# A decoder trunk on one core: the split of a state-space quarter moved behind the scan's loops, and its 20 small transfers begun by POOL

## The chip, the cores and the metric

One core of one Trainium2 chip runs the whole program. The metric is the device time of one execution in microseconds (us), as the median of several runs. The engines are named as in the profile: PE (TensorE, matrix products; PEld its weight loads), DVE (VectorE), ACT (ScalarE), POOL (GpSimd) and SP (SyncE, which in this kernel begins nearly all transfers; SPq is its queue).

## The reference

One layer of a decoder trunk over 1024 tokens and 1024 channels in float32. One projection of the normed input feeds three mixers, whose results are gated, summed and projected; a gated feed-forward block follows. The change touches only the state-space mixer:

```python
def s5_mixer(u, lam_re, lam_im, b_re, b_im, c_re, c_im, d_skip, log_dt, w_glu):
    ...
    lam_bar = jnp.exp(lam * dt)
    b_bar = ((lam_bar - 1.0) / lam)[..., None] * b
    bu = jnp.einsum('bsgh,gph->bsgp', uf.astype(jnp.complex64), b_bar)
    ...
    _, states = lax.associative_scan(combine, (a, bu), axis=1)
    y = jnp.einsum('bsgp,ghp->bsgh', states, c).real + d_skip * uf
    y = jax.nn.gelu(y.reshape(bsz, seq, SSM_WIDTH)).astype(u.dtype)
    y_lin, y_gate = jnp.split(y @ w_glu, 2, axis=-1)
    return y_lin * jax.nn.sigmoid(y_gate)
```

There are 32 groups of 16 channels with 64 complex states each: 512 channels in all.

## The kernel before, in words

All large products run in float32r as three matrix products: each operand is split into a high part (made by ACT, L61) and a low part (made by DVE as the difference, L62), and high x high, low x high and high x low are summed (L120, L122, L124). Weights arrive as `raw`, begun by SP at L83, and are split into `whi` and `wlo`; up to three weight blocks are split ahead of use. Nearly all tiles of 128 x 1024 floats share one pool of 44 pages.

The state-space mixer works in four quarters (q = 0 to 3) of 8 groups. For each, `s5` (L1102 and on) calls these steps:

- `s5_kernel`: PE makes the 8-step kernel (L979), ACT and DVE write it into `kz` (L983, L987), and 8 transfers (L991, 64 KB each) spread it into the page M.
- `s5_carry`: 4 transfers (L968, 128 KB each) move the coefficients into the page cp.
- `s5_back` (from q = 1 on): 8 transfers (L1084, 64 KB each) bring the result of the quarter before from DRAM into the page yT, with the time steps regrouped.
- `s5_inputs`: PE transposes (L1002), ACT writes the page Bm (L1005).
- `s5_parts` (from q = 1 on): ACT and DVE split yT into `mhi` and `mlo`, for the product with `w_glu` at the very end of the stage.
- `s5_scan`: PE makes the inputs of the states (L1015); DVE and ACT copy them to the page V (L1024, L1022); DVE makes products and sums (L1031 to L1035) and eight scans (L1039), then the state page X (L1048 to L1054), which POOL has cleared in its first column (L1044).
- `s5_tables` of the next quarter on DVE, then `s5_out`: PE sums M x U (L1066) and cp x X (L1070), ACT applies GELU (L1073), and SP begins the store `sy` (L1076).

Beside the quarters runs a filler, a generator that yields after each large matrix product: first the short convolution (`conv_rows`), whose blocks give `cb` (L719), `z` (L722), a POOL product of both (L726), `cy` on ACT and DVE (L727 to L729), and a second POOL product (L734); then the last input block (`u_block(3)`, `ut` at L683), then the mixing products of convolution and attention (`mix_plain`), whose sums DVE evacuates at L1166 and adds at L1170. `fill(n)` takes n steps of it; within the scan's loops `beat` takes 3.5 steps at a time, 5 in the last quarter. After the drain of the filler comes `mix_ssm`, which reads the four pairs `mhi`, `mlo` of the quarters.

In this stage PE runs in the written order (`manual_schedule`). The order on the other engines is chosen by a planner when the program is made; each engine then runs its instructions in that order, each waiting for its data. A tile's page comes free when its last reader is done. POOL begins no transfer in the kernel before.

```python
    def beat(self):
        self.due += self.F5B
        self.fill(int(self.due))
        self.due -= int(self.due)
...
    with tc.manual_schedule(engines={mybir.EngineType.PE}):
        k.fill(24)
        k.s5()
        k.drain()
```

Of the kernel before, what the change touches and what calls it, by code (L numbers as in the profile page):

```python
# [15 lines left out]
P = 128  # L16
# [17 lines left out]
class Trunk:  # L34
# [203 lines left out]
    def kv_rows(self):  # L238
# [7 lines left out]
        W = [self.weights() for _ in range(5)]  # L246
        A, B = (W[0], W[2]), (W[1], W[3], W[4])
        for t in range(NT):
            ps = self.wide()
            tok = slice(t * P, (t + 1) * P)  # L250
            for k in range(KD):
                a, b = A[k // 4], B[k // 3]
                ca, cb = slice((k % 4) * 256, (k % 4) * 256 + 256), slice((k % 3) * 280, (k % 3) * 280 + 280)
# [16 lines left out]
            nc.vector.tensor_tensor(sq[:, :256], kr, kr, op=OP.mult)  # L270
            nc.vector.tensor_reduce(self.ssk[:, t], sq[:, :256].rearrange("p (n d) -> p n d", d=64), axis=AX.X, op=OP.add)
            if t > 4:
# [34 lines left out]
    def q_rows(self):  # L307
# [3 lines left out]
        for t in range(NT):  # L311
# [8 lines left out]
            nc.vector.tensor_tensor(sq, q, q, op=OP.mult)  # L320
            nc.vector.tensor_reduce(self.ssq[:, t], sq.rearrange("p (n d) -> p n d", d=64), axis=AX.X, op=OP.add)
            self.q.append(q)
# [41 lines left out]
    def compress(self):  # L364
# [27 lines left out]
        for which in range(2):  # L392
# [25 lines left out]
            nc.vector.tensor_tensor(sv, kv, kv, op=OP.mult)  # L418
            nc.vector.tensor_reduce(ss, sv, axis=AX.X, op=OP.add)
            self.rstd(ss)  # L420
# [39 lines left out]
    def cmp_scores(self, t):  # L460
# [11 lines left out]
        m, sm = st[:, 0:8], st[:, 8:16]  # L472
        nc.vector.tensor_reduce(m, v, axis=AX.X, op=OP.max)
        nc.vector.tensor_tensor(v, v, m[:, :, None].to_broadcast([P, 8, 32]), op=OP.subtract)
        nc.scalar.activation(v, v, AF.Exp)
        nc.vector.tensor_tensor(v, v, self.seen[:, t, None, :].to_broadcast([P, 8, 32]), op=OP.mult)
        nc.vector.tensor_reduce(sm, v, axis=AX.X, op=OP.add)
        nc.vector.tensor_scalar(sm, sm, 1e-30, None, op0=OP.max)
# [110 lines left out]
    credit, t = 0.0, 0  # L589
# [88 lines left out]
    def u_block(self, q, beside=None):  # L678
# [9 lines left out]
        nc.sync.dma_start(spill, ut)  # L688
        self.U[q] = U = self.page("UT").rearrange("p (g n) -> p g n", g=8)
        nc.sync.dma_start(U, spill.rearrange("(g h) j n -> (h j) g n", g=8))  # L690

    def u_blocks(self):

        self.tab, self.U = {}, {}

# [267 lines left out]
    def s5_carry(self, cr):  # L963

        cp = self.page("cp").rearrange("p (a g c) -> p a g c", a=4, g=2)
        for c in range(2):
            for g in range(2):
                self.nc.sync.dma_start(cp[c * 64:(c + 1) * 64, :, g].rearrange("p a (d h) -> p a d h", h=16),  # L968
                                       cr[c][g * 64:g * 64 + 64, :, 0:8])
        return cp  # L970

    def s5_kernel(self, q, cr, bb):

        nc = self.nc
        M = self.page("M").rearrange("p (a g c) -> p a g c", a=4, g=2)
        ps = self.acc()
        for a in range(4):
            for c in range(2):
                nc.tensor.matmul(ps[:32, a * P:(a + 1) * P], bb[:, c, a].rearrange("p g h -> p (g h)"),  # L979
                                 cr[c][:, a, 1:9].rearrange("p d h -> p (d h)"), start=c == 0, stop=c == 1)  # L980
        kz = self.page("kz")[:32, :960].rearrange("p (a c) -> p a c", a=4)
        nc.gpsimd.memset(kz[:, :, 128:240], 0.0)
        nc.scalar.activation(kz[:, :, 0:128], ps[:32].rearrange("p (a c) -> p a c", a=4), AF.Copy)  # L983
        dd = self.half("dd")[:32, :64].rearrange("p (a h) -> p a h", a=4)
        nc.vector.tensor_tensor(dd, self.eye2[:, None, :].to_broadcast([32, 4, 16]),
                                self.dT[:, 4 * q:4 * q + 4, None].to_broadcast([32, 4, 16]), op=OP.mult)
        nc.vector.tensor_tensor(kz[:, :, 112:128], kz[:, :, 112:128], dd, op=OP.add)  # L987
        for g in range(2):
            for a in range(4):
                x = kz[g * 16:(g + 1) * 16, a]  # L990
                nc.sync.dma_start(M[:, a, g], bass.AP(x.tensor, x.offset, [list(x.ap[0]), [16, 8], [1, P]]))  # L991
        self.fill(self.F5)
        return M

    def s5_inputs(self, q, bp):

        nc = self.nc
        B = self.page("Bm").rearrange("p (a g c s) -> p a g c s", a=4, g=2, c=2)
        ps = self.wide()
# [4 lines left out]
        for c in range(2):  # L1004
            nc.scalar.activation(B[:, :, :, c], ps.rearrange("p (j c g s) -> p c j g s", j=4, c=2, g=2)[:, c], AF.Copy)  # L1005
        self.fill(2 * self.F5)
        return B

    def s5_scan(self, q, U, B, ep):
        nc = self.nc  # L1010
        v = nc.vector
        V = self.page("V5").rearrange("p (c a n) -> p c a n", c=2, a=4)
        ps = self.wide()
        for j in range(8):
            nc.tensor.matmul(ps[:, j * P:(j + 1) * P], B[:, j // 2, j % 2].rearrange("p c s -> p (c s)"), U[:, j],  # L1015
                             start=True, stop=True)
        pv = ps.rearrange("p (a g n) -> p g a n", a=4, g=2)
        for g in range(2):
            for c in range(2):
                o = V[g * 64:(g + 1) * 64, c]  # L1020
                if c:
                    nc.scalar.activation(o, pv[c * 64:(c + 1) * 64, g], AF.Copy)  # L1022
                else:
                    nc.vector.tensor_copy(o, pv[c * 64:(c + 1) * 64, g])  # L1024
        self.fill(2 * self.F5)
        f = lambda x: x.rearrange("p a n -> p (a n)")
        vr, vi, ec, es = f(V[:, 0]), f(V[:, 1]), f(ep[:, 0]), f(ep[:, 1])
        t = [self.half("m5") for _ in range(3)]
        a, b = self.half("a5"), self.half("b5")
        for o, z, x0, x1, op in ((b, t[2], vi, vr, OP.subtract), (a, t[0], vr, vi, OP.add)):  # L1030
            v.tensor_tensor(z, x0, ec, op=OP.mult)  # L1031
            self.beat()
            v.tensor_tensor(t[1], x1, es, op=OP.mult)
            self.beat()
            v.tensor_tensor(z, z, t[1], op=op)  # L1035
            self.beat()
            for j in range(4):
                s = slice(j * P, (j + 1) * P)
                v.tensor_tensor_scan(o[:, s], self.mag8[:, 4 * q + j:4 * q + j + 1].to_broadcast([P, P]), z[:, s], 0.0,  # L1039
                                     op0=OP.mult, op1=OP.add)  # L1040
                if j % 2:
                    self.beat()
        X = self.page("X5").rearrange("p (a g n) -> p a g n", a=4, g=2)
        nc.gpsimd.memset(X[:, :, :, 0:1], 0.0)  # L1044
        w = lambda x: x.rearrange("p (a n) -> p a n", a=4)[:, :, 0:127]
        ec, es = ep[:, 0, :, 0:127], ep[:, 1, :, 0:127]
        for c, x0, x1, op in ((0, a, b, OP.subtract), (1, b, a, OP.add)):
            v.tensor_tensor(w(t[0]), w(x0), ec, op=OP.mult)  # L1048
            self.beat()
            v.tensor_tensor(w(t[1]), w(x1), es, op=OP.mult)  # L1050
            self.beat()
            for g in range(2):
                pr = slice(g * 64, g * 64 + 64)
                v.tensor_tensor(X[c * 64:(c + 1) * 64, :, g, 1:], w(t[0])[pr], w(t[1])[pr], op=op)  # L1054
                self.beat()
        return X

    def s5_out(self, q, U, M, X, cp):

# [18 lines left out]
    def s5_back(self):  # L1078

        nc, spill = self.nc, self.spill_y  # L1080
        yT = self.page("yT").rearrange("p (t n) -> p t n", t=8)
        back = spill.rearrange("(t h) g n -> t g h n", t=8)
        for t in range(8):
            nc.sync.dma_start(yT[:, t], back[7 - t])  # L1084
        self.last = yT

    def s5_parts(self):
# [14 lines left out]
    def s5(self):  # L1102
        self.yT = []
        tab = self.tab
        for q in range(4):
            bp, cr, bb, ep = tab.pop(q)
            M = self.s5_kernel(q, cr, bb)
            cp = self.s5_carry(cr)
            U = self.U[q]
            if q:  # L1110
                self.s5_back()
            B = self.s5_inputs(q, bp)
            if q:
                self.s5_parts()
            self.F5B = 3.5 if q < 3 else 5
            X = self.s5_scan(q, U, B, ep)
            if q < 3:
                for _ in self.s5_tables(q + 1, tab):
                    self.beat()
            self.fill(self.F5S)  # L1120
            self.s5_out(q, U, M, X, cp)
        self.fill(16)
        self.s5_back()
        self.fill(16)
        self.s5_parts()
# [661 lines left out]
```

## Time and profile before

| | |
|---|---|
| median of 3 runs | 1776.4 us (1775.83 to 1778.55) |
| profiled execution | 1776.64 us, of which the span from first to last instruction is 1774.7 us |
| mean granted clock of PE in the span | 0.993 of full speed |
| busy share of the span | PE 98%, PEld 81%, DVE 68%, ACT 45%, POOL 6% |
| transfers | 189.78 MB, mean 107 GB/s |
| the state-space stage | about 640 to 960 us |

All times in the rows are microseconds from the span's start. A row of the timeline gives start, duration, engine, line, operation, output<-inputs and shapes; in square brackets stands how long the engine sat idle before it and what released it. A granted clock of 1.00 is 2.4 GHz, 0.50 is 1.2 GHz.

### The profile page before, as it was taken

Reading aid. Unit: us, or ns where it says so; the run is one execution under the profiler, and the core shown is the slowest. Engines: PE = TensorE matmul, PEld = TensorE weight load, DVE = VectorE, ACT = ScalarE, POOL = GpSimd, SP = SyncE. Lnnn points to the kernel's source line nnn. Section 1 sums busy time; section 2 is a strip of 40 time slices with the busy share of each in tenths; the row PEclk is TensorE's granted clock in tenths of the full one; section 3 lists DMA queues with packets and bytes.
Section 4 is the critical chain, followed back from the end, with each engine's and each line's share of the span. In section 5 each row is a group of like instructions: output and inputs, shape, how many; then the busy total and the mean of one; then the engine's idle time right before and its main releaser. Section 6 shows DMA issues by size and latency. Waiting matters only on the chain.

```text
span 1774.7 us, 23597 instructions
## 1 busy us (share of the span) xinstructions
PE 1736.4 (98%) x8637; PEld 1437.0 (81%) x8637; DVE 1202.1 (68%) x2414; ACT 794.7 (45%) x1477; POOL 108.8 (6%) x94
## 2 busy tenths in 40 slices
PE   8999999999999999998979999999999999999999
PEld 7987788888888888887868888778888888888887
DVE  6975456667666674485675687698667776688681
ACT  6415567777777742233122234642323233244360
POOL 0000000000000010111000000002112211120000
PEclk9999999999999999999989999999999999999999
DMA  4213322221211224213636322433322332477531
GB/s 170 73 42 110 120 78 66 60 60 48 58 40 57 60 66 128 66 42 95 222 122 213 107 95 80 164 119 119 102 101 95 114 107 89 165 259 264 160 95 48
DMA packets 172665, 189.78 MB, mean 107 GB/s; under 512 B 16938, under 2 KB 129670, under 8 KB 172550
## 3 DMA queue, kind: packets, MB, share of 16 engines
q1 hardware_dynamic: 172517, 188.27, 33.1%
q8 instruction: 68, 1.11, 0.2%
q14 instruction: 48, 0.39, 0.1%
q10 hardware_dynamic: 32, 0.01, 0.0%
HBM read 134.50 MB, written 47.45 MB: 103 GB/s over the span
## 4 chain that ended last, share of the span: by engine, by line
PE 76%; DVE 12%; ACT 4%; issue 2%; SPq 2%; DMA 2%; POOL 1%; POOLq 0%; ACTq 0%; DVEq 0%
PE wide L1517 11%; PE acc L120 10%; PE acc L124 10%; PE acc L122 10%; PE acc L1517 7%; PE acc L1624 5%; PE wide L1624 5%; PE acc L560 3%; PE wide L519 3%; PE acc L1286 2%; DVE A L62 2%; PE wide L1286 2%; PE acc L583 2%; PE acc L582 2%; PE wide L257 1%
## 5 line engine op out<-in xcount | busy, mean ns | idle before, releaser
L120 PE MATMUL acc<-hh,whi 128*128 128x512 f32 x672 | 269.6, 401 | 4.8 <-ACT whi L61 3.3
L124 PE MATMUL acc<-hh,wlo 128*128 128x512 f32 x672 | 268.3, 399 | 1.7 <-DVE wlo L62 1.7
L122 PE MATMUL acc<-hl,whi 128*128 128x512 f32 x672 | 268.8, 400 | 0.0
L1517 PE MATMUL wide<-B,A 128*128 128x512 f32 x1056 | 250.7, 391 | 0.3
L1517 PEld LDWEIGHTS wide<-B,A 128*128 128x128 f32 x1056 | 196.6, 188 | 47.1 <-DVE sg L1530 3.3
L1517 PE MATMUL acc<-B,A 128*128 128x512 f32 x792 | 192.0, 393 | 2.6 <-ACT A L61 1.6
L1517 PEld LDWEIGHTS acc<-B,A 128*128 128x128 f32 x792 | 148.8, 189 | 35.6 <-ACT A L61 2.4
L120 PEld LDWEIGHTS acc<-hh,whi 128*128 128x128 f32 x672 | 127.1, 189 | 26.0 <-ACT whi L61 3.7
L124 PEld LDWEIGHTS acc<-hh,wlo 128*128 128x128 f32 x672 | 127.3, 189 | 22.2 <-DVE wlo L62 2.8
L122 PEld LDWEIGHTS acc<-hl,whi 128*128 128x128 f32 x672 | 127.1, 189 | 19.6 <-issue 0.2
L61 ACT ACTIVATE A<-S 128x512 fp32r<-128x512 f32 x88 | 54.8, 627 | 164.7 <-DVE S L1449 164.0
L62 DVE TENSOR_TENSOR ptl<-acc,pth 128x512 fp32r<-128x512 f32 (+1 forms) x152 | 93.8, 619 | 50.3 <-ACT pth L61 49.1
L1624 PE MATMUL acc<-wdp,act 128*128 128x512 f32 x528 | 121.5, 389 | 0.6 <-DVE wdp L62 0.6
L524 DVE CUSTOM_DVE_ANT_0 p<-wide,mask 128x640 f32<-128x640 f32 (+7 forms) x128 | 90.1, 704 | 43.2 <-PE wide L519 40.5
L62 DVE TENSOR_TENSOR wlo<-raw,whi 128x1024 fp32r<-128x1024 f32 (+1 forms) x75 | 90.5, 1210 | 40.0 <-ACT whi L61 24.4
L1624 PEld LDWEIGHTS acc<-wdp,act 128*128 128x128 f32 x528 | 99.0, 188 | 21.7 <-DVE wdp L62 1.0
L1473 POOL TENSOR_TENSOR sg<-sg 128x512 f32<-128x512 f32 x44 | 73.9, 1680 | 598.2 <-ACT A L61 520.4
L527 ACT ACTIVATE p<-p,small 128x640 f32<-128x640 f32 (+7 forms) x128 | 93.6, 731 | 37.0 <-DVE small L524 34.9
L120 PE MATMUL acc<-mhi,whi 128*128 128x512 f32 x256 | 101.8, 398 | 7.3 <-DVE m L1166 7.3
L122 PE MATMUL acc<-mlo,whi 128*128 128x512 f32 x256 | 101.8, 398 | 4.1 <-DVE mlo L62 4.1
L61 ACT ACTIVATE pth<-acc 128x512 fp32r<-128x512 f32 (+1 forms) x152 | 80.9, 534 | 46.0 <-PE acc L560 45.4
L124 PE MATMUL acc<-mhi,wlo 128*128 128x512 f32 x256 | 101.3, 396 | 0.0
(397 smaller groups left out, 3246.1 us busy)
## 6 DMA issues: line engine op xcount, KB each, us to landing
raw<-in_ffn_w_gate_up_dram SPq DMA_DIRECT2D x52, 512.0 KB
raw<-in_w_in_dram SPq DMA_DIRECT2D x48, 512.0 KB
sa<-sg SPq DMA_DIRECT2D x77, 256.0 KB
araw<-sa SPq DMA_DIRECT2D x77, 256.0 KB
sg<-tg SPq DMA_DIRECT2D x48, 256.0 KB
gp<-sg SPq DMA_DIRECT2D x24, 512.0 KB
x<-in_x_dram SPq DMA_DIRECT2D x16, 512.0 KB
wd<-in_ffn_w_down_dram SPq DMA_DIRECT2D x11, 512.0 KB
```

Source lines behind the costliest of these rows:

```text
L61: self.nc.scalar.activation(hi, src, AF.Copy)
L62: self.nc.vector.tensor_tensor(lo, src, hi.bitcast(F32), op=OP.subtract)
L120: self.nc.tensor.matmul(out, hi(k), mh(k), start=start and j == 0, stop=False)
L122: self.nc.tensor.matmul(out, hi(k), ml(k), start=False, stop=False)
L124: self.nc.tensor.matmul(out, lo(k), mh(k), start=False, stop=stop and j == n - 1)
L519: nc.tensor.matmul(ps[:, c * 512:c * 512 + w], self.QS[t][:, h], k[:, k0 + c * w:k0 + c * w + w], start=z == 0, stop=z == 1)
L524: nc.vector.tensor_tensor_reduce(p[:, :n].rearrange("p (c w) -> p c w", c=pieces), v, m.rearrange("p (c w) -> p c w", c=pieces), scale=-1. ...
L527: nc.scalar.activation(p[:, :n], p[:, :n], AF.Exp, scale=-1.0, bias=st[:, hh:hh + 1], accum_out=st[:, 2 + hh:3 + hh])
L1286: nc.tensor.matmul(ps, act[:, x * 512 + t * P:x * 512 + (t + 1) * P], w[:, y * 512:y * 512 + 512], start=i == 0 and j == 0 and p in (1, 5, ...
L1473: e.tensor_tensor(o, x, y, op=op)
L1517: nc.tensor.matmul(ps, x, y, start=p in (1, 5, 6, 7) and k + j == 0, stop=k == 3 and j == 2, skip_group_check=True)
L1624: nc.tensor.matmul(ps, act[:, x * 512 + t * P:x * 512 + (t + 1) * P], w[:, y * 512:y * 512 + 512], start=i == 0 and j == 0 and p in (1, 5, ...
```

## The change

In `s5`, the state inputs are made before the transfers of `s5_back` are written, and `s5_parts` moves from before `s5_scan` into it, behind the loops with the eight scans and ahead of the page X. The 8 transfers of `s5_kernel`, the 4 of `s5_carry` and the 8 of `s5_back` are begun by POOL in place of SP, in all four quarters.

```diff
@@ s5_carry
         for c in range(2):
             for g in range(2):
-                self.nc.sync.dma_start(cp[c * 64:(c + 1) * 64, :, g].rearrange("p a (d h) -> p a d h", h=16),
+                self.nc.gpsimd.dma_start(cp[c * 64:(c + 1) * 64, :, g].rearrange("p a (d h) -> p a d h", h=16),
                                        cr[c][g * 64:g * 64 + 64, :, 0:8])
@@ s5_kernel
         for g in range(2):
             for a in range(4):
                 x = kz[g * 16:(g + 1) * 16, a]
-                nc.sync.dma_start(M[:, a, g], bass.AP(x.tensor, x.offset, [list(x.ap[0]), [16, 8], [1, P]]))
+                nc.gpsimd.dma_start(M[:, a, g], bass.AP(x.tensor, x.offset, [list(x.ap[0]), [16, 8], [1, P]]))
         self.fill(self.F5)
@@ s5_scan
                                      op0=OP.mult, op1=OP.add)
                 if j % 2:
                     self.beat()
+        if q:
+            self.s5_parts()
         X = self.page("X5").rearrange("p (a g n) -> p a g n", a=4, g=2)
@@ s5_back
         for t in range(8):
-            nc.sync.dma_start(yT[:, t], back[7 - t])
+            nc.gpsimd.dma_start(yT[:, t], back[7 - t])
         self.last = yT
@@ s5
             U = self.U[q]
+            B = self.s5_inputs(q, bp)
             if q:
                 self.s5_back()
-            B = self.s5_inputs(q, bp)
-            if q:
-                self.s5_parts()
             self.F5B = 3.5 if q < 3 else 5
             X = self.s5_scan(q, U, B, ep)
```

## Rows read from the trace of the kernel before

**Rows 1.** The page, part 1: busy time of PE over the whole span.

```profile
PE 1736.4 (98%) x8637; PEld 1437.0 (81%) x8637; DVE 1202.1 (68%) x2414; ACT 794.7 (45%) x1477; POOL 108.8 (6%) x94
```

**Rows 2.** Busy time by stretch: busy of each engine, PEclk, DMA share, GB/s.

```profile
core 0: us, PE busy (x) PEld busy (x) DVE busy (x) ACT busy (x) POOL busy (x), PEclk, DMA share, GB/s
820.00:840.00 20.00, 15.00 (x55) 11.34 (x54) 17.65 (x23) 8.91 (x10) 5.06 (x6) 0.83 0.21 72
...
900.00:920.00 20.00, 14.29 (x43) 11.14 (x44) 18.05 (x31) 3.68 (x4) 0.11 (x1) 0.70 0.54 185
```

**Rows 3.** PE's waits, 640 to 1050 us: total us, times, longest.

```profile
PE acc L120 <- DVE m L1166: 7.3, 2, 6.2
PE acc L122 <- DVE mlo L62: 4.1, 1, 4.1
PE acc L120 <- ACT whi L61: 3.3, 1, 3.3
PE acc L124 <- DVE wlo L62: 1.7, 1, 1.7
```

**Rows 4.** Busy time by stretch, from PE's restart to full clock after each long wait.

```profile
826.40:833.55 7.15, 5.42 (x12) 3.78 (x13) 7.05 (x7) 3.68 (x5) 4.85 (x6) 0.52 0.35 114
901.63:905.16 3.53, 3.53 (x9) 2.74 (x9) 3.53 (x7) 2.45 (x3) 0.11 (x1) 0.51 1.00 350
909.87:915.48 5.61, 5.61 (x14) 4.42 (x14) 4.14 (x8) 0.00 (x0) 0.00 (x0) 0.51 0.34 123
```

**Rows 5.** Timeline, third quarter (q = 2), on PE, DVE, ACT and POOL.

```profile
809.61 1.95 PE L1015 MATMUL wide<-UT,Bm 128*128 128x128 f32 x16
...
826.40 0.64 PE L120 MATMUL acc<-hh,whi 128*128 128x512 f32 x1 [3.28 <-ACT whi L61]
...
822.21 1.98 DVE L62 TENSOR_TENSOR mlo<-yT,mhi 128x1024 fp32r<-128x1024 f32 x1 [18.13 <-ACT mhi L61]
824.11 0.67 DVE L1024 COPY V<-wide 64x512 f32<-64x512 f32 x1
...
820.13 2.05 ACT L61 ACTIVATE mhi<-yT 128x1024 fp32r<-128x1024 f32 x1 [7.25 <-DMA yT<-sy]
822.09 1.14 ACT L727 ACTIVATE cy<-z,par 128x1024 f32<-128x1024 f32 x1
...
825.31 1.04 ACT L61 ACTIVATE whi<-raw 128x1024 fp32r<-128x1024 f32 x1
...
812.96 2.39 POOL L726 TENSOR_TENSOR z<-z,cb 128x1024 f32<-128x1024 f32 x1 [17.44 <-ACT z L722]
```

**Rows 6.** Timeline of SP's queue, third quarter: transfers begun.

```profile
804.14 6.24 SPq L991 DMA_DIRECT2D M<-kz  x8
810.48 2.64 SPq L968 DMA_DIRECT2D cp<-cr  x4
813.22 4.99 SPq L1084 DMA_DIRECT2D yT<-sy  x8
```

**Rows 7.** L991 over all quarters: ns min/median/max, first and last start.

```profile
L991 SPq DMA_DIRECT2D M<-kz x32: 581/597/1728, 679.2 to 880.5; - x32
```

**Rows 8.** Timeline, fourth quarter (q = 3), on SP, ACT, DVE and PE.

```profile
876.04 5.10 SPq L991 DMA_DIRECT2D M<-kz  x8
...
885.19 5.32 SPq L1084 DMA_DIRECT2D yT<-sy  x8
...
892.53 2.06 ACT L61 ACTIVATE mhi<-yT 128x1024 fp32r<-128x1024 f32 x1 [13.43 <-DMA yT<-sy]
...
916.52 0.67 DVE L1054 TENSOR_TENSOR X<-m,m 64x508 f32<-64x508 f32 x1
...
922.10 1.40 DVE L1054 TENSOR_TENSOR X<-m,m 64x508 f32<-64x508 f32 x2
...
926.81 1.06 PE L1070 MATMUL wide<-X,cp 128*128 128x128 f32 x8
```

**Rows 9.** Timeline of ACT behind the fourth quarter: its split, and the first `mix_ssm` evacuation.

```profile
944.19 2.05 ACT L61 ACTIVATE mhi<-yT 128x1024 fp32r<-128x1024 f32 x1 [10.71 <-DMA yT<-sy]
...
960.32 0.60 ACT L1192 ACTIVATE tgp<-acc 128x512 f32<-128x512 f32 x1 [12.18 <-PE acc L124]
```

## The prediction

> **What bounds the kernel now.** I read the page's busy times first: TensorE (PE) is busy 98% of the span [rows 1], so a change of the state-space stage pays only where PE stands still or runs at a lower clock. Next the busy times by stretch, for the stage from 640 to 960 us: PE is full in every stretch but a few, of which two stand here, 5.0 us short at a mean clock of 0.83 and 5.7 us short at 0.70 [rows 2]. Then PE's own waits in that stage. There are four rows: 7.3 us for evacuations by L1166 (6.2 and 1.1), 4.1 for a low part, 3.3 for a high part and 1.7 for another low part, 16.4 us in all [rows 3]. After each long one PE works at half clock for a while: busy 5.42 us at 0.52, 3.53 at 0.51, 5.61 at 0.51 [rows 4]. Busy time times the missing share of the clock is 2.6 + 1.7 + 2.75 = 7.1 us. So 23.4 us of the stage is PE's loss, and no change here can give back more.
>
> Where does it come from? In the third quarter (q = 2) the state matrix product L1015 ends at 809.6 + 1.95 = 811.6, yet VectorE (DVE) copies it at 824.11 only, because the split of the quarter before (high part on ScalarE, ACT, at 820.13; low part on DVE, idle 18.1 us before it) stands ahead of it, waiting for the 8 transfers of L1084 [rows 5]. On ACT the high part `whi` that PE needs at 823.1 (826.40 less 3.28) stands behind the same split and behind `cy`, and is made at 825.31 [rows 5]. On SP the 8 transfers begin at 813.22, behind 8 of L991 and 4 of L968 [rows 6]. The fourth quarter has the same picture: the split's high part at 892.53, with the evacuations and the low part that PE waited for behind it [rows 3, 8]. I read the ordering so: a page is given out in the order in which the program first writes pages, so what is written in the program after `mhi`, `mlo` is also placed after them on its engine, ready or not.
>
> **The change, part by part.**
>
> *The split behind the scan's loops.* It removes no instruction. Ahead of the split now stand the copies of L1015's result, the six products and sums and the eight scans of `s5_scan`, and all filler emitted with them. For PE this is 16 + 50 filler products in the fourth quarter; `mhi` moves from about 882 to some 15 us later in PE's time. So in the fourth quarter the evacuations and the low parts that PE waited for no longer stand behind it: 10.3 us of waits [rows 3] and 1.7 + 2.75 of clock [rows 4], 14.7 us. The wait of 1.1 us is DVE's backlog from the same cause, and I count it as gone.
>
> *What is late next in that quarter* is the scan's own result, X, which now stands behind the split. It needs an issue price.
>
> *20 transfers a quarter from SP to POOL.* No row shows POOL beginning a transfer. The nearest rows are SP's for the same transfers: 0.6 us in the median and 1.73 at most [rows 7], and 4.99 for 8 [rows 6]. Below 0.64 nothing suggests a POOL that is quicker than SP, and above 1.73 I have no row. No row is nearer to one end than to the other, so I take their geometric middle, **1.05 us** a transfer, 21.0 us for 20. The Trainium skill ("DMA: Bandwidth & Descriptors", Latency and other measured facts) gives about 1 us to the first byte for a transfer begun by POOL and 0.6 for one begun by SP; adding its difference to SP's price would make 1.04 and the same sum. No run here shows it yet.
>
> For the fourth quarter: POOL begins at 876.04, is through at 897.0; the last landing is 2.0 us behind the last issue, as on SP, where the eighth issue ended at 885.19 + 5.32 = 890.5 and the split began at 892.53 [rows 8]. High part 2.05 and low part 1.98 [rows 5] end at 903.1. X's last part took from 916.5 to 923.5 with all that lay between [rows 8], 7.0 us, so 910.1. L1070 reads X at 926.81 [rows 8], less 14.7 us is 912.1. It fits by 2 us. For evacuations that still queue behind it I take off 2.0, three of L1166's.
>
> *What is queued behind them on POOL.* This speaks against the change. In the third quarter POOL's product L726 ran at 812.96 for 2.39 us, then `cy` on ACT (1.14), then `whi` (1.04) [rows 5]. The 8 transfers of `s5_back` stand ahead of that product in the program, and so now on POOL: 804.14 + 21.0 = 825.1. Product until 827.5, `cy` until 828.7, `whi` until 829.7: PE goes on at 829.75 and not at 826.40, **3.35 us later**. The 1.7 us for the low part and the half clock stay as they are. The bounds: at 0.64 us a transfer `whi` is there at 821.5, before PE wants it, and this wait is gone; at 1.73 it is there at 843.4, 17 us later than now.
>
> *Edits at nothing.* The state inputs' product ahead of `s5_back` (Bm no longer written behind yT): PE waited for no Bm [rows 3]; if that cover fails, its copies of about 1 us. M and cp, 12.6 us on POOL: their readers L1066, L1070 come 30 us and more later in each quarter. SP gets 13 us a quarter back: PE waited for no load [rows 3], so no gain; a loss of the same size is excluded only as long as POOL's packets don't hold up the loads. POOL's other product (L734) in the second quarter slips by up to 21 us; its result is read by a mixing product many blocks later, and PE waited for nothing in that quarter. The last quarter's result: its split starts at 944.19, mixing with it begins 2.7 us before the first evacuation at 960.32 [rows 9]; 8 issues at 1.05 cost 3.4 us of the 9 between the split's end and that start.
>
> **Sum.** -14.7 + 2.0 - 1.1 + 3.35 = -10.4 us. The profiled execution took 1776.64 us (span 1774.7 and 1.9 around it), 0.2 above the median of the runs, 1776.4. Forecast: 1776.64 - 10.4 = **1766.2 us**.
>
> **Rivals.**
> - *Cheap issues.* If POOL needs 0.64 to 0.8 us, the third quarter's wait goes too: at 0.64 all 23.4 us return, 1753.2; at 0.8 `whi` is there at 824.7, and 14.7 + 1.1 + 1.5 = 17.3 make 1759.3. For it: these are the same plain transfers of 64 and 128 KB. Against it: it is another engine, and nothing shows it as quick as SP.
> - *Late POOL (the slower side).* Place: the third quarter's product L726 behind 20 transfers. Each 0.1 us of price costs 2 us there, and from 1.15 on also 2 us at X in the fourth quarter, whose spare 2 us are then used up. At 1.6: L726 starts at 836.1, `whi` ends at 840.7, +14.3; X is ready at 921.1, 9.0 late, so 5.7 of the 14.7 remain; with the 1.1, +7.5, **1784.1**. It decides from about 1.4 us on, where the sum is nought. For it: the price is unknown, and DVE, which stood idle there before [rows 5], now works while POOL issues. The Trainium skill ("SBUF — State Buffer", SBUF: two separate sides) says that POOL cannot write a transfer's descriptors while DVE holds the port that both share; by that rule the issues would lengthen in this way. No run here shows it.
> - *The order does not move.* If the planner still places the split ahead of L1024's copies, because the data seem ready to it, the waits stay and the data land later: 804.14 + 21.0 + 2.0 = 827.1 for 820.13 in the third quarter, 899.0 for 892.53 in the fourth. +7.0 and +6.5 at the two PE stalls: 1790.1. For it: engines do run instructions ahead of the written order in this trace. Against: in the rows the copies stand behind the split with their data ready for 12 us [rows 5], which readiness on the chip cannot explain and page order can.
>
> **How the numbers follow.** What a measurement of this kernel can tell from no change is 0.2%, 3.6 us. Forecast 0.48 (prices 0.85 to 1.3; its own range is 1760 to 1774, and 0.04 of it lies within 0.2%), cheap issues 0.18, late POOL 0.24 (0.09 of it within 0.2%, 0.15 slower), order unmoved 0.10. Faster: 0.44 + 0.18 = 0.62; same: 0.04 + 0.09 = 0.13; slower: 0.15 + 0.10 = 0.25. The range goes from the cheap end, 1753, to the late case, 1784, and leaves out the unmoved order and the worst of late POOL, some 0.16.
>
> **What would show it.** In the profile after, DVE's L1024 copies should stand ahead of the low part of yT in the second to fourth quarter and start when L1015 ends; the waits of PE for L1166 (6.2) and for mlo (4.1) should be gone and the clock near 0.9 to 1.0 there. POOL's pitch between two transfers gives the price. L726 in the third quarter should start at the last of the 20 transfers, and PE's wait for `whi` should be about 6.6 us in place of 3.3. The forecast is wrong if that wait is gone (cheap), if it passes 13 us or PE waits for X at L1070 (late), or if yT's split still stands ahead of the copies.

## The result, and the profile after

| | before | after |
|---|---|---|
| median, first set of runs (4 each) | 1776.12 us | 1758.38 us (1757.11 to 1759.28) |
| ratio, 95% interval | | 0.9898 [0.9881, 0.9915] |
| a later set (9 and 4 runs) | 1774.63 us | 1756.03 us, ratio 0.9892 [0.9879, 0.9906] |
| profiled execution, span | 1776.64, 1774.7 us | 1757.11, 1755.1 us |
| PE's waits, 640 to 1050 us | 16.4 us [rows 3] | 3.7 us |

The kernel became 17.7 us faster by the medians and 19.5 by the two profiled executions. The forecast was 10.4.

First the page: busy times (beside [rows 1]), and the transfers of the queue that is new.

```profile
PE 1730.0 (99%) x8637; PEld 1433.0 (82%) x8637; DVE 1207.2 (69%) x2414; ACT 795.0 (45%) x1477; POOL 154.6 (9%) x174
...
q0 software_dynamic: 3328, 6.31, 1.8%
```

POOL has 80 instructions more, the 20 transfers of four quarters, and 45.8 us more busy time: 0.57 us each, which is their pitch, since a row overlaps the next a little. PE's own busy time fell by 6.4 us with the same 8637 products, near the 7.1 that [rows 4] cost at half clock. Now PE's waits of the stage (beside [rows 3]), and the two stretches of [rows 2]:

```profile
PE acc L120 <- DVE m L1166: 1.8, 1, 1.8
PE acc L120 <- DVE gp L1166: 1.5, 1, 1.5
PE acc L124 <- DVE wlo L62: 0.4, 2, 0.2
```

```profile
820.00:840.00 20.00, 19.60 (x86) 15.57 (x84) 19.88 (x27) 9.27 (x11) 6.06 (x6) 1.00 0.23 79
900.00:920.00 20.00, 20.00 (x106) 17.17 (x105) 13.61 (x17) 1.97 (x2) 4.00 (x7) 1.00 0.39 122
```

Of 23.5 us of loss (16.4 of waits and 7.1 of clock; the forecast wrote 23.4), 3.7 are left at a granted clock of 1.00. So 19.8 are returned, and the profiled times are 19.5 apart. Where the time came from is in the timeline, first of the third quarter (beside [rows 5]), then of the fourth and what follows it (beside [rows 8, 9]):

```profile
809.77 1.95 PE L1015 MATMUL wide<-UT,Bm 128*128 128x128 f32 x16
...
811.75 0.69 DVE L1024 COPY V<-wide 64x512 f32<-64x512 f32 x1 [7.51 <-PE wide L1015]
...
816.37 3.24 DVE L1035 TENSOR_TENSOR m<-m,m 128x512 f32<-128x512 f32 x1
...
825.63 2.01 DVE L62 TENSOR_TENSOR mlo<-yT,mhi 128x1024 fp32r<-128x1024 f32 x1
...
820.13 1.04 ACT L61 ACTIVATE whi<-raw 128x1024 fp32r<-128x1024 f32 x1
...
821.70 2.13 ACT L61 ACTIVATE mhi<-yT 128x1024 fp32r<-128x1024 f32 x1
...
805.15 4.19 POOL L991 DMA_DIRECT2D M<-kz  x8 [9.47 <-issue]
809.26 2.54 POOL L968 DMA_DIRECT2D cp<-cr  x4
811.86 4.76 POOL L1086 DMA_DIRECT2D yT<-sy  x8
816.56 2.48 POOL L726 TENSOR_TENSOR z<-z,cb 128x1024 f32<-128x1024 f32 x1
...
877.37 4.80 POOL L1086 DMA_DIRECT2D yT<-sy  x8
...
894.86 2.00 DVE L62 TENSOR_TENSOR mlo<-yT,mhi 128x1024 fp32r<-128x1024 f32 x1
...
903.02 1.40 DVE L1056 TENSOR_TENSOR X<-m,m 64x508 f32<-64x508 f32 x2
...
915.86 4.83 POOL L1086 DMA_DIRECT2D yT<-sy  x8 [26.62 <-DVE gp L1166]
...
927.85 2.06 ACT L61 ACTIVATE mhi<-yT 128x1024 fp32r<-128x1024 f32 x1 [15.39 <-DMA yT<-sy]
...
932.60 0.50 PE L120 MATMUL acc<-mhi,whi 128*128 128x512 f32 x1 [1.51 <-DVE gp L1166]
```

The reader is to see four things. The copies of L1015's result start as L1015 ends, 12.4 us earlier than before, and the low part stands behind them. The 20 transfers of the third quarter are begun in 11.4 us (805.15 to 816.56), so L726 and with it `whi` come early: `whi` starts at 820.13 where it started at 825.31, and PE waits for it no more. X is done at 904.4, before PE reads it at 905.8. And the last quarter's split starts 7.2 us behind its last issue (915.86 + 4.83 = 920.7 to 927.85); before, it was 2.0.

The price of an issue, per line over all quarters (ns min/median/max, first and last start), and the landings (KB each, median us from issue to landing):

```profile
L991 POOL DMA_DIRECT2D M<-kz x32: 524/554/693, 680.0 to 874.4; - x32
...
L968 POOL DMA_DIRECT2D cp<-cr x16: 615/677/711, 684.6 to 876.8; - x16
...
L1086 POOL DMA_DIRECT2D yT<-sy x32: 582/627/694, 750.4 to 920.0; - x32
```

```profile
M<-kz POOLq DMA_DIRECT2D x32, 64.0 KB, 3.4
cp<-cr POOLq DMA_DIRECT2D x16, 128.0 KB, 4.2
...
yT<-sy POOLq DMA_DIRECT2D x32, 64.0 KB, 4.8
```

POOL needs 554 ns for what took SP 597 [rows 7].

### The profile page after: what moved, and what is told of

Same layout as the page of the kernel before. It is cut to its first block, busy times and chain, and to the rows that moved or that the text cites. A ratio compares the mean times of both kernels' runs of the same rounds, so it can differ in the third digit from the quotient of the medians.

```text
span 1755.1 us, 23643 instructions
## 1 busy us (share of the span) xinstructions
PE 1730.0 (99%) x8637; PEld 1433.0 (82%) x8637; DVE 1207.2 (69%) x2414; ACT 795.0 (45%) x1477; POOL 154.6 (9%) x174
## 4 chain that ended last, share of the span: by engine, by line
PE 85%; DVE 7%; ACT 4%; issue 1%; DMA 1%; POOL 0%; SPq 0%; POOLq 0%; DVEq 0%; ACTq 0%
PE wide L1517 13%; PE acc L120 11%; PE acc L124 11%; PE acc L122 11%; PE acc L1517 9%; PE acc L1624 6%; PE wide L1624 5%; PE acc L560 3%; PE wide L519 3%; PE acc L1286 2%; PE wide L1286 2%; PE acc L583 2%; PE acc L582 2%; PE wide L257 1%; PE wide L256 1%
## 5 line engine op out<-in xcount | busy, mean ns | idle before, releaser
L122 PEld LDWEIGHTS acc<-hl,whi 128*128 128x128 f32 x672 | 126.7, 188 | 19.7 <-issue 0.2
```

Source lines behind the costliest of these rows:

```text
L122: self.nc.tensor.matmul(out, hi(k), ml(k), start=False, stop=False)
```

## The experiments

The table gives the ratio to the kernel before on the same chip, and PE's waits from 640 to 1050 us in the profile.

| version | median us | ratio, 95% interval | PE's waits |
|---|---|---|---|
| order alone, all 20 on SP | 1753.92 | 0.9878 [0.9864, 0.9891] | 2.4 |
| the same again | 1753.01 | 0.9873 [0.9858, 0.9887] | 2.0 |
| POOL alone, old order | 1781.70 | 1.0037 [1.0025, 1.0049] | 21.0 |
| state inputs alone | 1775.70 | 0.9997 [0.9988, 1.0006] | 16.0 |
| V in half pages, old order | 1771.66 | 0.9973 [0.9964, 0.9982] | 14.1 |
| split moved in the fourth quarter alone | 1760.31 | 0.9917 [0.9904, 0.9931] | 5.4 |
| after, result on SP, M and cp on POOL | 1752.80 | 0.9873 [0.9858, 0.9888] | 1.8 |
| after, again | 1756.03 | 0.9892 [0.9879, 0.9906] | 4.4 |
| after, POOL's price made 1.02 us | 1768.76 | 0.9961 [0.9947, 0.9975] | 13.8 |
| after, 40 issues for 20 | 1781.27 | 1.0037 [1.0025, 1.0050] | 23.8 |
| after, result on SP, more filler | 1753.54 | 0.9875 [0.9859, 0.9892] | 2.3 |

### The two halves of the change, each alone

The kernel after with its transfers back on SP:

```diff
-                self.nc.gpsimd.dma_start(cp[...
+                self.nc.sync.dma_start(cp[...
-                nc.gpsimd.dma_start(M[:, a, g], ...
+                nc.sync.dma_start(M[:, a, g], ...
-            nc.gpsimd.dma_start(yT[:, t], back[7 - t])
+            nc.sync.dma_start(yT[:, t], back[7 - t])
```

> The kernel after with its 20 transfers a quarter back on SP: the split's new place alone. Order theory (the split's place carries the gain; POOL only spares SP some 13 us a quarter that nobody waits for): 1757 to 1762 us, PE's waits for L1166 (6.2) and for mlo gone, the waits left under 6 us. Rival (SP's relief carries a good part, because transfers on SP come late): 1766 to 1772 us, with waits of PE for loads or for the scan's result that the kernel after doesn't have.

The kernel before with the opposite edit, its three lines from `sync` to `gpsimd`:

> The kernel before with only the 20 transfers a quarter begun by POOL. Order theory: the split stands ahead of the copies of L1015's result as before, so the four waits of PE stay, 13 to 20 us in all, and the time is 1772 to 1782 us; since the transfers land later behind POOL's issue, rather above 1776 than below. Rival (SP's relief carries the gain): 1758 to 1766 us.

The order alone gives 1753.92 us, the whole gain and some more, and below the 1757 to 1762 that was expected; POOL alone costs 0.37%, some 6 us. The rival, that SP's relief pays, is out. PE's waits of POOL alone, beside [rows 3]:

```profile
PE acc L120 <- DVE m L1166: 7.8, 2, 6.7
PE acc L120 <- ACT whi L61: 4.9, 1, 4.9
PE acc L122 <- DVE mlo L62: 4.3, 1, 4.3
PE acc L120 <- DVE gp L1166: 2.3, 1, 2.3
PE acc L124 <- DVE wlo L62: 1.7, 1, 1.7
```

Each wait of before is there again, the one for `whi` longer by 1.6, since L726 now starts behind the transfers (819.18 for 812.96), and one of 2.3 for L1166 is new, in the last quarter. So the "late POOL" rival works already at a cheap price: 4.6 us more of waits, in an execution that was the fastest of its six (1778.54 us).

### The state inputs alone

```diff
+            B = self.s5_inputs(q, bp)
             if q:
                 self.s5_back()
-            B = self.s5_inputs(q, bp)
             if q:
                 self.s5_parts()
```

> The kernel before with only the state inputs' product placed ahead of the result's eight transfers; the split keeps its place. Theory: no PE wait goes, 1774 to 1779 us. Rival (the inputs' page behind yT's is what holds back the copies of L1015): 1758 to 1768 us.

0.9997, no difference. Of the order, then, it is the split's place that counts; this is by subtraction, since no run moved the split alone.

### Is it the page of V that held the copies back?

```diff
-        V = self.page("V5").rearrange("p (c a n) -> p c a n", c=2, a=4)
+        V = [self.half("V5").rearrange("p (a n) -> p a n", a=4) for _ in range(2)]
...
-                o = V[g * 64:(g + 1) * 64, c]
+                o = V[c][g * 64:(g + 1) * 64]
...
```

> The kernel before with one thing changed: the copy of the state matrix product's result is kept in two half pages instead of a page of the large pool; the split keeps its written place. Page-order theory (the copies stood behind the split because a page of the large pool is given out in the order of first writes): the copies start when L1015 ends, at about 812 us in the third quarter in place of 824, PE's wait of 6.2 for L1166 and of 4.1 for mlo go, and the time is 1758 to 1766 us without any change of the written order. Rival (the written order itself, or the data's readiness, holds them back): the copies stay at about 824 and the time is 1774 to 1779 us.

One half of the theory holds and the other falls, and 1771.66 us lies in neither expected range. The copies moved without any change of the written order, by 12.3 us in the third quarter. But PE's long waits did not go; DVE and PE of this version, third and fourth quarter:

```profile
811.78 0.68 DVE L1024 COPY V<-wide 64x512 f32<-64x512 f32 x1 [7.51 <-PE wide L1015]
...
881.30 0.68 DVE L1024 COPY V<-wide 64x512 f32<-64x512 f32 x1 [2.68 <-PE wide L1015]
...
893.59 1.95 DVE L62 TENSOR_TENSOR mlo<-yT,mhi 128x1024 fp32r<-128x1024 f32 x1 [9.73 <-ACT mhi L61]
...
899.74 0.77 PE L120 MATMUL acc<-mhi,whi 128*128 128x512 f32 x1 [6.45 <-DVE m L1166]
...
907.38 0.79 PE L122 MATMUL acc<-mlo,whi 128*128 128x512 f32 x1 [3.31 <-DVE mlo L62]
```

The copies are done at 883.9, yet DVE stands idle for 9.7 us before the low part of yT, and behind that low part come the evacuations by L1166 that PE waits for. The harm is the split's own place on DVE, not what its pages do to V. That V's copies were held back by the pool of V's page is shown, and V's copies were never the price: this version gains 0.27%, 4.2 us. By PE's waits and clock some 2.7 us of it come from 820 to 860 us (the wait for `whi` is 1.4 us in place of 3.3, and the clock from 820 to 840 us is 0.91 in place of 0.83), the rest from the fourth quarter. The rule by which the planner orders is not shown. In the third quarter of this version DVE runs L1031 and L1033 ahead of the split, but the sum L1035 only behind it, at 824.64, though its inputs are done at 816.7, it writes its half page in place and DVE stands idle for 6.1 us; an order of pages does not explain that.

### The forecast's first term by itself

The version with all on SP, and the split behind the loops in the fourth quarter alone:

```diff
-        if q:
+        if q == 3:
             self.s5_parts()
         X = self.page("X5")...
...
             if q:
                 self.s5_back()
+            if q in (1, 2):
+                self.s5_parts()
```

> The kernel after with its 20 transfers on SP and the split behind the scan's loops in the fourth quarter alone; in the second and third it stands ahead of the scan as before. Theory (the forecast's first term, 14.7 us of waits and half clock from the fourth quarter, and the backlog's 1.1): PE keeps waits of about 3.3 for whi and 1.7 for wlo near 823 and no others over 2; 1759 to 1763 us. Rival (the three quarters' waits hang together, so that part of them comes back elsewhere): 1764 to 1772 us.

1774.63 less 1760.31 is 14.3 us, and the two profiled executions, 1776.64 and 1760.50, are 16.1 apart. The forecast's term was 14.7; of the backlog's 1.1 us 0.8 are gone here too, which makes 15.5 by the rows. What is left are the third quarter's two waits, as expected:

```profile
PE acc L120 <- ACT whi L61: 3.0, 1, 3.0
PE acc L124 <- DVE wlo L62: 2.1, 1, 2.1
PE acc L120 <- DVE m L1168: 0.3, 1, 0.3
```

From here to the order in all quarters is 0.39% to 0.44% more (its two runs), 6.9 to 7.8 us. By the rows it is less: PE's waits fall from 5.4 to 2.4 and 2.0, of which 1.8 for L1166 is new (0.3 here), and 2.6 of clock come back, about 6 us in all. So 1 to 2 us of this step are not accounted for.

### What POOL costs in the kernel after

The eight transfers of `s5_back` alone back on SP, and the kernel after beside it on the same chip:

```diff
-            nc.gpsimd.dma_start(yT[:, t], back[7 - t])
+            nc.sync.dma_start(yT[:, t], back[7 - t])
```

> The kernel after with the eight result transfers a quarter back on SP, M's eight and cp's four still on POOL. Theory (POOL costs by the later landing of the result: the last quarter's high part starts 4.9 us later than with all on SP): 1752 to 1756 us, PE's wait of 1.5 for gp gone. Rival (it costs by what stands behind the 20 on POOL, or by DVE's longer work beside them): 1757 to 1760 us.

> The kernel after, unchanged, beside the three others on one chip: 1757 to 1760 us if its distance to the version with all transfers on SP is real, 1753 to 1756 us if that distance was between chips.

1752.80 us (runs of 1751.8 to 1753.4) against 1756.03 (1754.2 to 1757.3): the result's transfers cost 3.2 us on POOL, M's and cp's nothing that can be measured. 1756.03 falls between the two expectations for the repeat, and the repeat of all on SP on the same chip, further down, is 3.0 us below it; so the distance is real. The last quarter of the faster version, on ACT and in SP's queue:

```profile
922.95 2.06 ACT L61 ACTIVATE mhi<-yT 128x1024 fp32r<-128x1024 f32 x1 [10.90 <-DMA yT<-sy]
...
916.03 4.95 SPq L1086 DMA_DIRECT2D yT<-sy  x8
```

SP issues at the same pitch as POOL and ends at 921.0, 0.3 us later than POOL did, but the data are there 4.9 us sooner. In the kernel after, DVE's low part then stands in the way of L1166, and PE waits 1.5 us at 932.60; here that wait is gone. PE's waits in all are 1.8 us here and 3.7 and 4.4 in the two profiles of the kernel after, so they account for 1.9 to 2.6 of the 3.2. Why the same eight transfers land later from POOL's queue was not tried.

### The price that the forecast took

Two ways to make POOL slower. The first begins each transfer as two halves (for yT):

```diff
-            nc.gpsimd.dma_start(yT[:, t], back[7 - t])
+            for k in (0, 64):
+                nc.gpsimd.dma_start(yT[k:k + 64, t], back[7 - t][k // 16:k // 16 + 4])
```

> The kernel after with each of its 20 transfers a quarter begun as two halves, 40 issues in place of 20: the price of one transfer, which the forecast took as 1.05 us, is made so. Theory (the forecast's mechanism with its price): 40 issues at 0.53 to 0.6 us take some 22 us in the third quarter, L726 starts at about 827 in place of 816.6, whi ends at about 831, PE waits 6 to 9 us for it and works at half clock for some us after; the last quarter's result comes some 5 us later as well. 1766 to 1776 us. Rivals: a half costs half (the price goes by rows, not by issues), or POOL has room for it: 1757 to 1760 us.

POOL and the waits of PE in that version (its L1171 is L1166):

```profile
808.19 8.88 POOL L994 DMA_DIRECT2D M<-kz  x16 [10.79 <-issue]
816.91 4.52 POOL L969 DMA_DIRECT2D cp<-cr  x8
821.28 9.70 POOL L1091 DMA_DIRECT2D yT<-sy  x16
830.99 2.35 POOL L726 TENSOR_TENSOR z<-z,cb 128x1024 f32<-128x1024 f32 x1
```

```profile
PE acc L120 <- ACT whi L61: 10.5, 1, 10.5
PE acc L120 <- DVE gp L1171: 6.6, 2, 4.2
PE wide L1076 <- issue: 2.4, 1, 2.4
...
```

A half costs as much as a whole: 40 issues take 22.8 us, 1.14 for each transfer of before. The whole gain is lost and more, 1781.27 us, above what was expected, because beside `whi` the evacuations by L1171 come late too, and PE stands still ahead of L1076, the reader of X. But this version also has twice the transfers to land. The second way adds none: products of a constant on POOL ahead of each issue.

```diff
+            for _ in range(2):
+                nc.gpsimd.tensor_tensor(yT[:, t], self.ident, self.ident, op=OP.mult)
             nc.gpsimd.dma_start(yT[:, t], back[7 - t])
```

> The kernel after, with products of a 128x128 constant on POOL ahead of its transfers (one ahead of each of M and cp, two ahead of each of yT; what they write the transfer overwrites), so that the 20 transfers of the third quarter take about 20 to 22 us of POOL in place of 11.4 without more transfers: the price of 1.05 us that the forecast took. The forecast's own sum: 10 us below the kernel before, 1763 to 1768 us, with PE waiting 5 to 8 us for whi and nowhere else over 2. Rival (the forecast also undercounted what a late POOL costs in the fourth quarter and behind it, as 40 issues suggest): 1770 to 1780 us, with waits of over 4 us in all for mlo, gp or X.

First transfer, last transfers and L726 of the third quarter, and PE's two long waits:

```profile
807.84 0.55 POOL L994 DMA_DIRECT2D M<-kz  x1 [6.77 <-issue]
...
827.12 1.21 POOL L1091 DMA_DIRECT2D yT<-sy  x2
828.34 2.36 POOL L726 TENSOR_TENSOR z<-z,cb 128x1024 f32<-128x1024 f32 x1
```

```profile
PE acc L120 <- ACT whi L61: 9.9, 1, 9.9
PE acc L120 <- DVE gp L1171: 3.2, 1, 3.2
```

The 20 transfers now take 20.5 us, 1.02 each, nearly the 1.05 of the forecast. The time is 6.8 us below the kernel before (1775.52 to 1768.76), between the two expectations: the forecast's 10.4 was 3.6 too kind at its own price. The wait for `whi` is 9.9 where it gave 6.6, since the first transfer starts 3.7 us later than in [rows 6] (807.84 for 804.14); the 3.2 of the last quarter it had covered with spare time.

### A version that tries for the rest

```diff
-            self.F5B = 3.5 if q < 3 else 5
+            self.F5B = (3.5, 3.5, 4.25, 5)[q]
```

> The version with the eight result transfers on SP and M's and cp's twelve on POOL, with more filler for PE between the vector steps of the third quarter (4.25 products a beat in place of 3.5): an attempt at the last wait of the stage, 1.8 us for L1166 near 846 and the half clock behind it, some 1.3 us. If that wait comes from vector work that runs ahead of its filler: 1749 to 1751.5 us, the wait gone. If the wait only moves to another place: 1752 to 1755 us.

> The version with all twenty on SP and the split behind the loops, beside the other on one chip: 1752 to 1755 us, within 2 us of the version with M and cp on POOL, so that only the result's eight transfers cost anything on POOL; 3 us or more above it if M's and cp's place on SP costs too.

1753.54 us: nothing is gained. The wait of 1.8 is gone and others came, in the fourth quarter. That the filler spent in the third quarter is missing there is the likely reason, but no run shows it:

```profile
PE acc L122 <- DVE mlo L62: 1.4, 1, 1.4
PE wide L1072 <- issue: 0.7, 1, 0.7
```

The repeat of the version with all on SP (1753.01) cannot be told from the one with M and cp on POOL. Both beat the kernel before by 1.27% and the kernel after by 0.2%.

## Why the prediction was right in sign and 7 to 9 us short

- **The split's first term, -14.7, held.** The fourth quarter alone gives 14.3 us by the medians, and in the kernel after PE is full from 900 to 920 us at clock 1.00.
- **The step that failed is the price of an issue on POOL, 1.05 us.** It measured 0.55 to 0.68 by line, with a mean pitch of 0.57. From bounds of 0.64 and 1.73 the geometric middle was taken, though the nearest row by kind, SP's median for the very same transfers, stood at the cheap end [rows 7]; the maximum of 1.73 was no row of the same weight. With it fell the term of +3.35: the third quarter's 3.3 + 1.7 of waits and 2.6 of clock are returned but for 0.4, a term of -7.2 in its place. That is 10.5 us, more than the whole error. By its own signs the forecast's sum was wrong here: it named the wait for `whi` being gone as the mark of cheap issues, and 1758.38 lies outside the 1760 to 1774 of its own case and within the 1753 to 1759 of the rival that it gave 0.18.
- **The term of +2.0** for evacuations still queued in the fourth quarter did not appear there; 1.5 us of the kind appeared in the last quarter, and that this is near 2.0 is luck. There the forecast had hidden later issues under 9 us of spare time up to the first row of the mixing [rows 9]. The spare time was the wrong one: what waits is L1166, queued on DVE behind the split's low part, and the delay is the landing, not the issue. Putting the eight transfers on SP returns 3.2 us.
- **The term of -1.1** for DVE's backlog was wrong in sign: 1.8 us remain near 848, also with all transfers on SP. With the third quarter's split in its old place this wait is 0.3, so the new order has made it longer. The four terms as the rows give them are -14.7 - 7.2 + 1.5 + 0.7 = -19.7, the profiled difference is -19.5.
- **X is in time**: done at 904.4, read at 905.8. That 1.4 us of spare time is near the forecast's 2 is luck, for another chain sets it. POOL was through at 882.2 (877.37 + 4.80), 14.8 us ahead of the 897.0 worked out, yet the low part started at 894.86, only 6.2 us ahead of the 901.1 that follows from it. Its high part was done at 890.7, and from there to 894.86 DVE works without a pause: the low part stood in DVE's queue, and the price of the issues no longer set the time.
- **The reading of the order** was half right. The copies stood behind the split because of the pool of V's page, as the half pages show, though the planner's rule itself stays open; but PE's waits come from the split's own place ahead of L1166's evacuations.
- **The rivals.** "Cheap issues" happened: at 0.64 us it gave 1753.2, at 0.8 1759.3, and 1758.38 was measured at 0.57. Of the 5.2 us above 1753.2 the later landing is 3.2, and the wait near 848 is 1.8. "The order does not move" fell with the first lines of the timeline. "Late POOL" was a true mechanism, and nearer than the forecast said: made to cost 1.02 us, POOL leaves 6.8 us of gain. A line through this and the 18.6 of 0.57 would reach nought near 1.3, an estimate; the forecast put the turn at about 1.4. At 1.14 the kernel is 6.6 us slower than before, but with twice the transfers, so the price alone is not to blame for that.
- **The edits at nothing**: the state inputs' place (0.9997) and M's and cp's transfers cost nothing, as said. SP's relief gave nothing, as said.

On the two rules that were weighed: POOL's later first byte (the Trainium skill, "DMA: Bandwidth & Descriptors", Latency and other measured facts) was taken there for a price of the issue. No row shows 0.4 us more per issue; what grew is the landing. That these are two things another page says (the Trainium skill, "Perfetto Trace Analysis", DMA Instruction — SWDGE (GPSIMD)): POOL's row ends when the descriptors are written, not when the data have moved. The trace agrees: rows of 0.63 us, landings of 4.8. The lock on the port shared by DVE and POOL ("SBUF — State Buffer", SBUF: two separate sides, of the Trainium skill) lengthened no issue: the eight of yT took 4.80 us in the fourth quarter, with DVE busy for 4.68 of them, and 4.83 in the last, with DVE busy for 2.0. No row tells whether DVE held the port meanwhile, so the rule itself was not put to the test.

## What to carry to other kernels

Ask of a piece of work that waits for data not only whether it is needed yet, but what stands behind it on its engine: here a split that nobody needed for 60 us and more held back evacuations, and its place in the order was worth all of the gain. When an issue moves to an engine that has not issued before, price it by the same transfer's median elsewhere, and price the landing apart from the issue; test what it would cost at twice that price, since the slope can be steep (9 us more of POOL in a quarter cost 11 to 12 us here). Test the parts of a change alone: one of two made this kernel slower, and the other hid it.

## What was not expected of the hardware

- POOL begins a plain transfer of 64 KB in 0.55 to 0.63 us, as SP does, and a half of it costs as much as the whole.
- The same eight transfers, issued at the same pitch and at the same time, are there 2.0 us after the last issue from SP (920.98 to 922.95) and 7.2 us after it from POOL (920.7 to 927.85). The reason stays open.
- With POOL alone in the old order, POOL stopped between two of its issues until an earlier transfer of its own had landed, 0.72 and 1.60 us in the third quarter; the kernel after has such a stop of 1.36 us in the second. The releaser is inferred by the profile:

```profile
816.40 0.59 POOL L1084 DMA_DIRECT2D yT<-sy  x1 [0.72 <-DMA cp<-cr]
818.58 0.58 POOL L1084 DMA_DIRECT2D yT<-sy  x1 [1.60 <-DMA cp<-cr]
```

- DVE's sum L1035 took 3.24 us beside POOL's product L726, which ran from 816.56 to 819.04; its median is 0.69. In [rows 5] DVE stood idle through that product, but the kernel before has the same elsewhere: L1031 took 2.85 us from 829.05 on, beside L734, which ran from 828.50 to 831.36. In both cases, and in the second quarter of the kernel after (L1033, 3.21 us), DVE's instruction ends 0.54 to 0.57 us after POOL's, as if most of it ran only then. No wait of PE is put down to it. It fits the rule of the shared port (the Trainium skill, "SBUF — State Buffer", SBUF: two separate sides), by which a DVE instruction with two SBUF inputs and a POOL instruction that reads SBUF exclude each other, and the one that starts second stands still. By the rows DVE's began second in the kernel before, but 0.19 us first at 816.37, and POOL's spans are rough.
